# Block 2, the latents' attention: exponentials left undivided, outputs multiplied by reciprocal sums

## Chip, cores and metric

One NeuronCore of a Trainium2 chip runs the whole kernel. The metric is the device time of one execution in microseconds (us); three runs of the kernel before took 2768.22, 2770.35 and 2776.49, median 2770.35 us. Five engines matter: PE (TensorE, matrix products; PEld is its weight load), DVE (VectorE), ACT (ScalarE), POOL (GpSimd) and SP, whose queue issues most transfers.

## What is computed

Two blocks, each two layers deep, on 512 rows of width 1024. The change touches the second block's attention of the 512 latent rows: a windowed attention of 8 heads (A, with a sink logit) and a neighbourhood attention of 4 heads (B, with a bias), both also over 256 context keys.

```python
# A: window_gqa_latent, block of 128 queries
p = softmax(concatenate([s_win, s_ctx, s_sink], -1))
out = p[..., :span] @ vb + p[..., span:span+256] @ vc      # the sink only adds to the sum
# B: neighbourhood_latent
p = softmax(concatenate([s_nb, s_ctx], -1))
out = p[..., :n_keys] @ vr + p[..., n_keys:] @ vc
o = concatenate([o_a, o_b, o_c], -1) @ w_out               # o_c: a convolution branch
```

A row of p is exp(s - max) divided by its sum. Dividing the row of exponentials before the product with the values, or dividing the row of the output after it, gives the same output.

## The kernel before

The program is one straight instruction stream for each engine. A planner takes the program's operations, with costs and due times from a model of its own, and writes the order in which each engine gets them; every engine then works through its order. So two operations near each other in the text can stand far apart on an engine.

In block 2 each layer first projects the latent rows, then runs the latents' attention, then multiplies its output with `w_out` and goes on to the experts. The attention's output `oT` (printed as `mx` in the trace) is laid out transposed: chunk k holds the 64 channels of each of two heads on 128 partitions, 512 latents along the free axis. Chunks 0 to 3 are stage A (L1680 to L1719), chunks 4 and 5 stage B (L1726 to L1769), chunks 6 and 7 the convolution branch, whose taps (`conv_taps`, L862 and L865) and end (`conv_out`) are spread between.

Stage A runs over 4 pairs of heads `p_`, 4 tiles `t` of 128 latents and 2 heads `hh`: 32 heads' tiles a layer. `queries` (L1665, L1666) splits a pair's queries in two parts. A head's tile is: scores in PSUM (`scores`, `pa`, two buffers), the sink's column (L1699), `softmax_rows` into one of three `P` buffers, transposes by PE into `pt` (two buffers), copies to `PT`, and the products with the values into another `pt` tile, copied to `oT` (L1718). A tile has 513 columns (t = 0 and 3) or 641 (t = 1 and 2). Stage B runs over 2 pairs, 4 tiles and 2 heads: 16 heads' tiles a layer of 768 columns; L1749 adds the bias and takes the maximum.

`softmax_rows` takes the row maximum (L468), the exponential with its sum (L471, ACT; the sum leaves by a small read of ACT's accumulator), the reciprocal (L473, DVE) and multiplies the row of P by it (`copy`, L135): in A always on DVE, in B on DVE for the first head and on POOL for the second (`EA`, `EB`).

`proj_out` turns each chunk of `oT` into two parts, `hTh` (L369, ACT) and `hTl` (L370, DVE), which PE multiplies with the weights. Products of chunk 5 have to wait for the last output copy of stage B. `pj` is a third pair of PSUM buffers, which projections, small transposes and `conv_out` use.

Of the kernel before, what the change touches and what calls it, by code (L numbers as in the profile page):

```python
# [86 lines left out]
def _build(tc, nc, st, a, out):  # L87
# [38 lines left out]
    def copy(o, i, scale=None, eng=None):  # L126
        if eng is None:
            flip[0] ^= 1
            eng = "av"[flip[0]]
        if eng == "a":  # L130
            A.activation(o, i, AF.Copy, scale=1.0 if scale is None else scale)
        elif scale is None:
            V.tensor_copy(o, i)  # L133
        else:
            (G if eng == "g" else V).tensor_scalar(o, i, scale, None, op0=OP.mult)  # L135
# [11 lines left out]
    def pj():  # L147
        return cur["ps"].tile([128, 512], F32, tag="j", name="pj", bufs=2)
# [315 lines left out]
    def softmax_rows(S_, nh, lo, hi, P, ng=None, eng="v"):  # L464

        if ng is None:
            ng = small([128, nh], f"ng{nh}")
            V.tensor_reduce(ng, S_[:, :, lo:hi], axis=AX, op=OP.max, negate=True)  # L468
        su = small([128, nh], f"su{nh}")
        for i in range(nh):  # L470
            A.activation(P[:, i, lo:hi], S_[:, i, lo:hi], AF.Exp, bias=ng[:, i:i + 1], accum_out=su[:, i:i + 1])  # L471
        rc = small([128, nh], f"rc{nh}")
        V.reciprocal(rc, su)  # L473
        for i in range(nh):
            copy(P[:, i, lo:hi], P[:, i, lo:hi], rc[:, i:i + 1], eng)

    def heads2(x):
        return lambda hd: x[64 * (hd % 2):64 * (hd % 2) + 64, hd // 2, :]
# [973 lines left out]
    class Open:  # L1452
# [36 lines left out]
        def queries(self):  # L1489

            l, W, hcT = self.l, a["w_in_2"][self.l], self.hcT
            self.qa = self.crow().rearrange("p (a b) -> p a b", b=CTX)
            for j in range(2):
                w = wtile(W, 256 * j, 256)
                for b in range(2):
                    copy(self.qa[:, 2 * j + b, :], proj_T(w, hcT, CTX, b), 0.125)
            w = wtile(W, 768, 256)
            for b in range(2):
                copy(self.qb[:, b, :], proj_T(w, hcT, CTX, b), 0.125)
            conv_in(l, W, hcT, CTX, self.cglu, self.cpair)  # L1500
            bg.append(conv_taps(l, CTX, self.cglu, self.cacc))
            tick(8)
# [24 lines left out]
    for l in range(NL):  # L1527
# [152 lines left out]
        for p_ in range(4):  # L1680
            g = (2 * p_) // 4
            q_ = queries(qa[p_ // 2][:, p_ % 2, :])
            for t in range(4):
                c0, c1 = max(0, t - 1), min(3, t + 1)
                nw = c1 - c0 + 1
                lo = 512 - 128 * nw
                PT = ll.tile([128, 2, 4, 128], F32, tag="PT", name="PT", bufs=3)
                P5 = ll.tile([128, 2, 128], F32, tag="P5", name="P5", bufs=2) if nw == 3 else None
                tq = None
                for hh in range(2):  # L1690
                    hd = 2 * p_ + hh
                    s_ = pa().rearrange("p a b -> p (a b)")
                    scores(s_[:, lo:512], q_[:, hh, :], t, *part(kA, g, 128 * c0, 128 * c1 + 128), False)
                    if t > 0:
                        mm(s_[:, lo:lo + 128], identb, MB["left"], False, t == 3)
                    if t < 3:
                        mm(s_[:, 384:512], identb, MB["causal"], False, True)
                    scores(s_[:, 512:768], q_[:, hh, :], t, *part(kC, g, 0, CTX), True)
                    V.tensor_copy(s_[:, 768:769], sink[:, 8 * l + hd:8 * l + hd + 1])  # L1699
                    P = Pl()  # L1700
                    softmax_rows(s_[:, :776].unsqueeze(1), 1, lo, 769, P.unsqueeze(1), None, EA[(2 * t + hh) % len(EA)])
                    tp = pt()
                    for c in range(4):
                        tr(tp[:, 128 * c:128 * c + 128], P[:, lo + 128 * c:lo + 128 * c + 128])
                    copy(PT[:, hh, 0:4, :].rearrange("p c q -> p (c q)"), tp, eng="a")
                    if nw == 3:
                        if tq is None:
                            tq = pt()
                        tr(tq[:, 128 * hh:128 * hh + 128], P[:, lo + 512:lo + 640])
                if nw == 3:  # L1710
                    copy(P5, tq[:, :256].rearrange("p (h q) -> p h q", h=2))
                o_ = pt()
                for i in range(nw + 2):
                    for hh in range(2):
                        vv = va[:, c0 + i, 64 * g:64 * g + 64] if i < nw else vca[:, i - nw, 64 * g:64 * g + 64]
                        mm(o_[64 * hh:64 * hh + 64, :128], vv, PT[:, hh, i, :] if i < 4 else P5[:, hh, :], i == 0, i == nw + 1,
                           tile_position=(0, 64 * hh))
                copy(oT[:, p_, 128 * t:128 * t + 128], o_[:, :128])  # L1718
                tick(1)  # L1719
        if last:  # L1720
            qb = late_q()
            kb, vb = late()
# [3 lines left out]
        for p_ in range(2):  # L1726
            tb = [row4()[:, :960].rearrange("p (r c) -> p r c", c=64) for _ in range(2)]
            for r in range(2):
                for hh in range(2):
                    if r:  # L1730
                        G.memset(tb[hh][64:128, 0, :], 0.0)
                    src = bass.AP(natr.tensor, natr.offset + ((l * 4 + 2 * p_ + hh) * 15) * 8192 + 63,
                                  [[127, 64], [8192, 15 - r], [1, 64]])
                    nc.sync.dma_start(tb[hh][64 * r:64 * r + 64, r:15, :], src)
            for hh in range(2):
                G.tensor_tensor(out=tb[hh], in0=tb[hh],
                                in1=C["nacol"].unsqueeze(1).to_broadcast([128, 15, 64]), op=OP.add)
            q_ = queries(qb[:, p_, :])
            kB = keys(kb[:, p_, :], nbk[:, 4 * p_:4 * p_ + 2, :], nbk[:, 4 * p_ + 2:4 * p_ + 4, :])
            kC = keys(kcb[:, p_, :], *kparts(CTX, "BC"[p_]))  # L1740
            for t in range(4):
                PT = [ll.tile([128, 8, 128], F32, tag="PT", name="PT", bufs=3) for _ in range(2)]
                for hh in range(2):
                    hd = 2 * p_ + hh
                    s_ = pa().rearrange("p a b -> p (a b)")
                    scores(s_[:, 0:512], q_[:, hh, :], t, *part(kB, hh, 0, S), True)
                    scores(s_[:, 512:768], q_[:, hh, :], t, *part(kC, hh, 0, CTX), True)
                    m2 = small([128, 2], "m2")
                    V.tensor_tensor_reduce(out=s_[:, 0:512], in0=s_[:, 0:512],  # L1749
                                           in1=tb[hh][:, 7 - 2 * t:15 - 2 * t, :].rearrange("p r c -> p (r c)"),  # L1750
                                           scale=1.0, scalar=-3e38, op0=OP.add, op1=OP.max, accum_out=m2[:, 0:1])
                    V.tensor_reduce(m2[:, 1:2], s_[:, 512:768], axis=AX, op=OP.max)
                    ng = small([128, 1], "ngd")
                    V.tensor_reduce(ng, m2, axis=AX, op=OP.max, negate=True)
                    P = Pl()
                    softmax_rows(s_[:, :776].unsqueeze(1), 1, 0, 768, P.unsqueeze(1), ng, EB[(2 * t + hh) % len(EB)])
                    for i in range(2):
                        tp = pt()
                        for c in range(3):
                            tr(tp[:, 128 * c:128 * c + 128], P[:, 384 * i + 128 * c:384 * i + 128 * c + 128])  # L1760
                        copy(PT[hh][:, 3 * i:3 * i + 3, :].rearrange("p c q -> p (c q)"), tp[:, :384], eng="av"[i])
                o_ = pt()
                for c in range(6):
                    for hh in range(2):
                        hd = 2 * p_ + hh
                        vv = vb[:, c, 64 * hd:64 * hd + 64] if c < 4 else vcb[:, c - 4, 64 * hd:64 * hd + 64]
                        mm(o_[64 * hh:64 * hh + 64, :128], vv, PT[hh][:, c, :], c == 0, c == 5,
                           tile_position=(0, 64 * hh))
                copy(oT[:, 4 + p_, 128 * t:128 * t + 128], o_[:, :128])  # L1769
        pop()  # L1770
        conv_out(l, S, acc, oT, 6, lambda: (t4(), t4()))
        pop()
# [50 lines left out]
```

## Time and profile before

| | us |
|---|---|
| median of three runs | 2770.35 |
| profiled execution, its own time | 2777.7 |
| its span in the trace | 2775.9 |
| PE busy / PE weight loads busy | 2406.4 / 1439.1 |
| DVE busy | 1224.7 |
| ACT busy | 801.2 |
| POOL busy | 508.8 |

The four stretches in which the changed code runs are, from the span's start: A of the first layer 1100 to 1177 us, B of the first layer 1177 to 1236, A of the second layer 2036 to 2145, B of the second layer 2145 to 2203. They are 303 us of the span. A line of the trace gives an operation's line in the kernel, its engine, the tile written <- the tiles read; PE's products of the helper `mm` all have line L151, PE's transposes L160, the copies of `copy` L131 (ACT) and L133 or L135 (DVE, POOL).

### The profile page before, as it was taken

The page shows a single profiled execution, that of the slowest core. Times are in us where ns is not written, and L with a number is a line of the kernel's source. Part 1 is how long each engine was busy: PE and PEld are TensorE (multiplying, and loading weights), DVE is VectorE, ACT ScalarE, POOL GpSimd, SP SyncE. Part 2 cuts the span into 40 slices and gives each one's busy share as a digit, 9 for nine tenths or more (in the row PEclk, how much of TensorE's full clock was granted, in tenths as well). Part 3 has the DMA queues.
Part 4 walks back from the last instruction along what each step waited for, and adds up shares of the span by engine and source line. Part 5 has one row for each costly group of instructions (what it writes and reads, how often), then busy time and mean ns, then how long its engine had stood idle before and what let it go on. Part 6 is the DMA issues. An engine that isn't in the chain of part 4 may idle for free.

```text
span 2775.9 us, 39464 instructions
## 1 busy us (share of the span) xinstructions
PE 2406.4 (87%) x16255; PEld 1439.1 (52%) x16255; DVE 1224.7 (44%) x2367; ACT 801.2 (29%) x1522; POOL 508.8 (18%) x389
## 2 busy tenths in 40 slices
PE   6988889988998887995999999995798959988887
PEld 5765667655677665774333333334576733333323
DVE  4423554423666977866010101028778661112213
ACT  3353332363334434742101010103337420000001
POOL 3101222011233234042001010104322420000001
PEclk9999999999999997997999999998999969999998
DMA  5353562354444124035899999982221459999996
GB/s 179 116 169 120 164 182 84 107 184 141 133 134 153 61 99 128 8 131 212 355 393 349 419 341 420 340 337 100 68 68 30 160 207 410 421 420 421 421 421 233
DMA packets 216746, 613.17 MB, mean 221 GB/s; under 512 B 37592, under 2 KB 110830, under 8 KB 170486
## 3 DMA queue, kind: packets, MB, share of 16 engines
q1 hardware_dynamic: 207142, 576.74, 55.8%
q0 software_dynamic: 5440, 20.45, 2.6%
q10 hardware_dynamic: 3984, 13.45, 1.2%
q8 instruction: 128, 2.10, 0.3%
q14 instruction: 52, 0.43, 0.0%
HBM read 581.92 MB, written 28.67 MB: 220 GB/s over the span
## 4 chain that ended last, share of the span: by engine, by line
PE 35%; DVE 13%; DMA 11%; issue 8%; ACT 2%; POOL 2%; DVEq 0%; POOLq 0%; ACTq 0%; SPq 0%
PE pm L151 20%; PE pj L151 5%; PE pa L151 5%; DMA w<-in_w_up_dram 4%; DMA w<-in_w_gate_dram 4%; DVE acc L865 3%; DMA w<-in_w_down_dram 2%; PE pt L151 2%; PE pt L160 1%; DVE wl L331 1%; PE ptm L160 1%; DVE s L245 1%; POOL lnst L249 1%; ACT P L471 1%; DVE ng L468 1%
## 5 line engine op out<-in xcount | busy, mean ns | idle before, releaser
L151 PE MATMUL pm<-w,q 128*64 128x512 f32 (+1 forms) x1600 | 359.5, 597 | 40.3 <-DMA w<-in_w_up_dram 27.6
L151 PE MATMUL pm<-w,xT 128*32 128x512 f32 x3072 | 338.7, 599 | 0.0
L151 PEld LDWEIGHTS pm<-w,q 128*64 128x64 f32 x1600 | 122.6, 141 | 265.3 <-issue 200.5
L329 ACT ACTIVATE wh<-w 128x1024 fp32r<-128x1024 f32 (+2 forms) x154 | 161.3, 1050 | 317.2 <-PE pj L151 106.7
L331 POOL TENSOR_TENSOR wl<-w,wh 128x1024 fp32r<-128x1024 f32 (+1 forms) x57 | 143.5, 2520 | 464.0 <-ACT wh L329 448.0
L151 PE MATMUL pj<-hTh,wh 128*128 128x512 f32 x512 | 215.8, 422 | 13.3 <-ACT ty L301 7.2
L151 PEld LDWEIGHTS pm<-w,xT 128*32 128x32 f32 x3072 | 104.4, 111 | 228.1 <-issue 223.6
L151 PE MATMUL pj<-hTl,wh 128*128 128x512 f32 x512 | 207.7, 406 | 0.0
L151 PE MATMUL pj<-hTh,wl 128*128 128x512 f32 x512 | 206.1, 406 | 0.0
L151 PE MATMUL pm<-w,hid 128*32 128x512 f32 x1536 | 178.5, 593 | 0.0
L331 DVE TENSOR_TENSOR wl<-w,wh 128x1024 fp32r<-128x1024 f32 (+2 forms) x97 | 132.4, 1366 | 102.7 <-ACT wh L329 102.1
L1276 DVE TENSOR_TENSOR q<-pm,q 128x512 f32<-128x512 f32 x24 | 16.6, 692 | 285.6 <-PE pm L151 285.6
L160 PE MATMUL pt<-ident,P 128*128 128x128 f32 x712 | 121.2, 290 | 13.0 <-DVE mx L133 4.8
L151 PE MATMUL pa<-wh,hTh 128*128 128x512 f32 x256 | 106.3, 416 | 22.4 <-DVE ty L963 15.1
L1276 DVE TENSOR_TENSOR ty<-pm,ty 128x512 f32<-128x512 f32 x16 | 11.1, 691 | 256.4 <-PE pm L151 256.4
L151 PEld LDWEIGHTS pj<-hTh,wh 128*128 128x128 f32 x512 | 100.7, 197 | 40.5 <-issue 8.9
L1180 POOL DMA_INDIRECT q<-rowsl,idx x16 | 15.4, 960 | 563.0 <-PE ptm L160 432.7
L151 PEld LDWEIGHTS pj<-hTh,wl 128*128 128x128 f32 x512 | 99.5, 194 | 26.0 <-issue 3.3
L151 PEld LDWEIGHTS pj<-hTl,wh 128*128 128x128 f32 x512 | 100.2, 196 | 24.7 <-issue 4.2
L468 DVE TENSOR_REDUCE ng<-pa 128x1 f32<-128x513 f32 (+5 forms) x124 | 93.4, 756 | 35.1 <-PE pa L151 33.1
L151 PEld LDWEIGHTS pm<-w,hid 128*32 128x32 f32 x1536 | 50.4, 110 | 112.5 <-issue 110.7
L865 DVE SCALAR_TENSOR_TENSOR acc<-glu,vec,acc 128x512 f32<-128x512 f32 x120 | 108.6, 946 | 0.1
(447 smaller groups left out, 4465.3 us busy)
## 6 DMA issues: line engine op xcount, KB each, us to landing
w<-in_w_gate_dram SPq DMA_DIRECT2D x128, 1024.0 KB
w<-in_w_up_dram SPq DMA_DIRECT2D x127, 1024.0 KB
w<-in_w_down_dram SPq DMA_DIRECT2D x118, 1024.0 KB
w<-in_w_mod_dram SPq DMA_DIRECT2D x96, 512.0 KB
w<-in_w_in_dram SPq DMA_DIRECT2D x94, 512.0 KB
w<-in_w_out_dram SPq DMA_DIRECT2D x40, 512.0 KB
w<-in_w_down_dram SPq DMA_DIRECT2D x16, 512.0 KB
z<-q ACTq DMA_DIRECT2D x8, 512.0 KB
```

The source lines that it names most:

```text
L151: return T.matmul(o, l, r, start=start, stop=stop_, skip_group_check=True, **kw)
L160: T.transpose(o, i, ident[: i.shape[0], : i.shape[0]])
L245: pin(V.bn_stats(s6[:, c, :], x[:, c * w:c * w + w]))
L249: pin(G.tensor_tensor(out=rs, in0=ve, in1=mhalf[:, :n], op=OP.pow))
L329: A.activation(hi, w, AF.Copy)
L331: (lo_eng or (G if lot[0] % 3 == 0 else V)).tensor_tensor(out=lo, in0=w, in1=hi.bitcast(F32), op=OP.subtract)
L468: V.tensor_reduce(ng, S_[:, :, lo:hi], axis=AX, op=OP.max, negate=True)
L471: A.activation(P[:, i, lo:hi], S_[:, i, lo:hi], AF.Exp, bias=ng[:, i:i + 1], accum_out=su[:, i:i + 1])
L865: V.scalar_tensor_tensor(acc[:, c, :n], glu[:, c, tap:tap + n], w, acc[:, c, :n], op0=OP.mult, op1=OP.add)
L1180: pin(G.indirect_dma_start(out=r, out_offset=None, in_=s["rows"][:], in_offset=bass.IndirectOffsetOnAxis(ap=s["idx"][:, i:i + 1], axis=0)) ...
L1276: V.tensor_tensor(out=x, in0=up[b][h], in1=x, op=OP.mult)
```

## The change

`softmax_rows` is replaced in both latents' stages by `exp_rows`, which does the maximum and the exponential alone and leaves the sum in one column of a small tile `su` of the pair. P stays undivided through the transposes and the products with the values. After a pair's four tiles `over_sums` takes the reciprocals of its eight columns of sums, spreads each over the 64 partitions of its head with a product (the stationary operand is a column of reciprocals repeated 64 times, the moving one the 128x128 unit matrix) into a `pj` tile, and multiplies the pair's chunk of `oT` with it in place. `EA` and `EB` no longer matter. The other attentions of the kernel keep `softmax_rows`.

```diff
+    def exp_rows(S_, lo, hi, P, ng, su):
+        if ng is None:
+            ng = small([128, 1], "ng1")
+            V.tensor_reduce(ng, S_[:, lo:hi], axis=AX, op=OP.max, negate=True)
+        A.activation(P[:, lo:hi], S_[:, lo:hi], AF.Exp, bias=ng, accum_out=su)
+
+    def over_sums(su, o):
+        rc = small([128, 4, 2], "rcp", bufs=2)
+        V.reciprocal(rc, su)
+        p = pj()
+        for t in range(4):
+            for hh in range(2):
+                mm(p[64 * hh:64 * hh + 64, 128 * t:128 * t + 128], rc[:, t, hh:hh + 1].to_broadcast([128, 64]), ident,
+                   True, True, tile_position=(0, 64 * hh))
+        V.tensor_tensor(out=o, in0=p, in1=o, op=OP.mult)
...
             q_ = queries(qa[p_ // 2][:, p_ % 2, :])
+            su = small([128, 4, 2], "suq", bufs=3)
...
-                    softmax_rows(s_[:, :776].unsqueeze(1), 1, lo, 769, P.unsqueeze(1), None, EA[(2 * t + hh) % len(EA)])
+                    exp_rows(s_, lo, 769, P, None, su[:, t, hh:hh + 1])
...
                 tick(1)
+            over_sums(su, oT[:, p_, :])
...
             q_ = queries(qb[:, p_, :])
+            su = small([128, 4, 2], "suq", bufs=3)
...
-                    softmax_rows(s_[:, :776].unsqueeze(1), 1, 0, 768, P.unsqueeze(1), ng, EB[(2 * t + hh) % len(EB)])
+                    exp_rows(s_, 0, 768, P, ng, su[:, t, hh:hh + 1])
...
                 copy(oT[:, 4 + p_, 128 * t:128 * t + 128], o_[:, :128])
+            over_sums(su, oT[:, 4 + p_, :])
```

## Rows read from the trace of the kernel before

**Rows 1.** Stretches: length, busy us (count) of PE, PEld, DVE, ACT, POOL; clock, DMA share, GB/s

```profile
1100.00:1177.00 77.00, 69.18 (x637) 54.58 (x636) 67.72 (x200) 52.40 (x122) 10.38 (x11) 0.94 0.07 14
1177.00:1236.00 59.00, 54.00 (x450) 42.93 (x446) 44.55 (x130) 30.58 (x63) 26.26 (x22) 1.00 0.21 67
2036.00:2145.00 109.00, 97.40 (x764) 80.04 (x764) 84.89 (x193) 65.80 (x140) 21.54 (x19) 0.95 0.22 48
2145.00:2203.00 58.00, 53.31 (x441) 42.50 (x442) 43.46 (x125) 30.39 (x63) 26.52 (x22) 1.00 0.21 69
```

**Rows 2.** Chain of waits, shares by line: first layer's A and B, second layer's A

```profile
by line: PE pa L151 21.6%; PE pt L151 16.1%; ACT P L471 12.1%; DVE ng L468 10.1%; DVE P L135 9.5%; PE pt L160 9.3%; issue 2.1%; DVE Q L1666 1.8%; DVE q L885 1.7%; DVE af L1054 1.4%; DVE rc L473 1.3%; DVE pa L1699 1.3%; ACT PT L131 1.3%; DVE
by line: PE pa L151 35.8%; PE pt L151 20.4%; PE pt L160 13.2%; DVE pa L1749 6.8%; issue 5.1%; DVE PT L133 4.4%; ACT hTh L369 2.2%; ACT P L471 2.0%; ACT q L887 1.7%; ACT PT L131 1.7%; DVE m L1752 1.4%; DVE P L135 1.2%; DVE q L885 1.0%; ACT m
by line: PE pj L151 27.0%; PE pa L151 18.4%; PE pt L151 13.0%; PE pt L160 9.3%; ACT P L471 5.6%; DVE P L135 5.4%; DVE ng L468 4.5%; DVE Q L1666 3.7%; issue 2.5%; DVE nbk L1648 2.3%; ACT PT L131 1.4%; PE pj L160 1.2%; DVE q L885 1.2%; DVE pa
```

**Rows 3.** Waits of PE: for whom, us in total, times, longest; first layer's A, B

```profile
PE pa L151 <- ACT P L471: 3.0, 8, 0.6
PE pj L160 <- DVE af L1054: 2.8, 1, 2.8
...
PE pt L160 <- DVE PT L133: 1.5, 4, 0.6
PE pa L151 <- ACT hTh L369: 1.0, 1, 1.0
```

**Rows 4.** Groups of instructions, first layer's A and B: busy, mean ns | idle before

```profile
L135 DVE TENSOR_SCALAR P<-P,rc 128x513 f32<-128x513 f32 x16 | 10.8, 676 | 0.4
L135 DVE TENSOR_SCALAR P<-P,rc 128x641 f32<-128x641 f32 x16 | 8.8, 551 | 0.5
L135 DVE TENSOR_SCALAR P<-P,rc 128x768 f32<-128x768 f32 x8 | 6.3, 782 | 0.2
L473 DVE RECIPROCAL rc<-su 128x1 f32<-128x1 f32 x48 | 7.4, 154 | 2.3 <-ACT P L471 1.7
...
L135 POOL TENSOR_SCALAR P<-P,rc 128x768 f32<-128x768 f32 x8 | 17.7, 2210 | 15.6 <-DVE rc L473 6.6 <-DVE ngd L1754 5.3 <-PE pt L151 2.2
```

**Rows 5.** Order of time at a change of pair in A: start, us, engine

```profile
1135.83 0.49 DVE L135 TENSOR_SCALAR P<-P,rc 128x513 f32<-128x513 f32 x1
1136.35 0.69 DVE L1666 TENSOR_TENSOR Q<-q,Q 64x512 fp32r<-64x512 f32 x1
1137.06 0.29 DVE L133 COPY mx<-pt 128x128 f32<-128x128 f32 x1
1137.41 0.88 PE L160 MATMUL pt<-ident,P 128*128 128x128 f32 x6 [0.18 <-DVE mx L133]
1138.61 0.39 PE L151 MATMUL pa<-KA,Q 128*128 128x256 f32 x1 [0.32 <-ACT P L471]
```

**Rows 6.** Order of time in A: DVE beside POOL

```profile
1143.15 2.24 POOL L1736 TENSOR_TENSOR q<-q,cst 128x960 f32<-128x960 f32 x1 [4.81 <-DMA q<-natr]
1143.23 2.44 DVE L135 TENSOR_SCALAR P<-P,rc 128x513 f32<-128x513 f32 x1
```

**Rows 7.** Order of time in the output product: DVE beside POOL

```profile
1243.56 2.52 POOL L964 TENSOR_TENSOR q<-q,ty 128x512 f32<-128x512 f32 x2
1243.92 0.69 DVE L963 TENSOR_TENSOR ty<-pa,q 128x512 f32<-128x512 f32 x1 [1.75 <-PE pa L151]
```

**Rows 8.** Order of time in A: bursts of PE, value products and transposes

```profile
1121.40 0.88 PE L151 MATMUL pt<-PT,va 128*64 128x128 f32 x12
1122.64 0.66 PE L160 MATMUL pt<-ident,P 128*128 128x128 f32 x4
```

**Rows 9.** Order of time at the end of B, first layer

```profile
1234.67 0.28 ACT L131 ACTIVATE mx<-pt 128x128 f32<-128x128 f32 x1 [2.25 <-PE pt L151]
1234.98 0.63 ACT L369 ACTIVATE hTh<-mx 128x512 fp32r<-128x512 f32 x1
1235.66 0.50 PE L151 MATMUL pa<-wh,hTh 128*128 128x512 f32 x1 [1.03 <-ACT hTh L369]
```

## Prediction before the run

> **What bounds the kernel now.** The change lives in four stretches that the windows of the trace bound: A and B of the first layer, 77 and 59 us, A and B of the second, 109 and 58 us, 303 us together [rows 1]. I read the busy times of these windows first. PE has something in flight for 69.18 of 77 us, 54.00 of 59, 97.40 of 109 and 53.31 of 58, that is 89 to 92%, 273.9 us in all; what it leaves empty is 7.8, 5.0, 11.6 and 4.7 us, 29.1 us. DVE is the second engine: 67.72 of 77 us (88%) in the first layer's A, 75 to 78% in the other three. ACT has 50 to 70%, POOL 14 to 46%.
>
> The second view is the chain of waits in these windows [rows 2]. Products and transposes of PE are the largest part of it, but in the first layer's A DVE's division of P (L135) carries 9.5%, its reciprocal (L473) 1.3% and the maximum (L468) 10.1%. In the second layer's A the division carries 5.4%, and the projections that are mixed in there (`pj`) 27.0%. In B it is 1.2%. The third view is PE's own list of waits [rows 3]: nowhere among its longer ones does PE wait for the division itself. It waits for the exponential that frees a score buffer (3.0 us in 8 waits in the first layer's A), for a copy of transposed P, for the last chunk before the output product (1.0 us). So DVE sits on the path through what stands behind the division in its order, not through P arriving late.
>
> **What the change removes.** In one layer 40 divisions on DVE, 10.8 + 8.8 + 6.3 = 25.9 us, and 48 reciprocals, 7.4 us [rows 4]; 33.3 us a layer, 66.6 us in two layers if the second costs the same. On POOL 8 divisions of 2210 ns, 17.7 us a layer. Most of that lies beside PE's work and is worth nothing. What can come back at most is what stands on the chain: (9.5 + 1.3)% of 77 = 8.3 us in the first layer's A, 5.4% of 109 = 5.9 in the second's, 1.2% of 59 = 0.7 in each B: 15.6 us. B's chain also has 5.1% of "issue", 3.0 us, of which a part can be a division that DVE holds without getting on; with all of it in both layers the upper end is 21.6 us. The lower end is 0, since PE is at 89 to 92%.
>
> Which value? At a change of pair in A the division of 0.49 us stands in front of the split of the next queries (0.69) and the output copy (0.29), and PE's transposes start when that copy is done [rows 5]. With reciprocal and division gone the copy comes about 0.6 us earlier. But PE showed waits of only 0.18 us in front of these transposes and 0.32 in front of the next scores: what is late next is PE's own work. So I don't take the whole chain: three quarters where DVE is at 88% (6.2 of 8.3), half in the second layer's A, where the projections fill PE (3.0 of 5.9), and all of B (1.4). Gain: 10.6 us.
>
> A division can cost far more than its 0.48 us: one took 2.44 us while POOL added the bias tables for 2.24 us, and both ended almost together [rows 6]. That is one of the places where the chain's 8.3 us come from. The Trainium skill says why (SBUF — State Buffer, section "SBUF: two separate sides"): DVE in a two-port mode and POOL take one pair of ports in turn, and the loser is held for the whole instruction; rows and page agree. The new multiplication reads one operand from PSUM, and an addition of that form took 0.69 us while POOL was busy for 2.52 us [rows 7], so I price it at 0.69 without such a wait.
>
> **What the change adds.** Six pairs a layer, 12 in all, each with one reciprocal of 8 columns, 8 products and one multiplication of 128x512.
>
> PE: the products have the shape of the value products (64 stationary columns, 128 moving ones, the two halves of the array in turn). Twelve of those took 0.88 us, 0.073 each; four transposes, which can't go in pairs, 0.66, 0.165 each [rows 8]. A set of 8 is then 0.59 us by the nearer row and 1.32 by the farther, 7.0 or 15.8 us for 12 sets. A stationary operand that repeats one column 64 times is in no row; its load is priced with the burst, as one of 64 different columns, and the farther row is the end if it is not. The lower end is 0, because PE leaves 29.1 us empty. The sets come due at the changes of pair, where PE does wait [rows 5], so I count half of the nearer value: 3.5 us. What is queued behind them on PE are the next pair's scores; they would wait for the reciprocal only if the planner put the set ahead of the last value products, since the sums are there before P has been transposed.
>
> DVE: 12 times (0.154 + 0.69) = 10.1 us against 66.6 removed, nothing on the path in A and between B's pairs, where 0.69 us go into the time made free. At the end of B there is no cover: the last output copy ends at 1234.95, and the cast for the output product starts at 1234.98 [rows 9], with PE idle for 1.03 us until it is done. The multiplication goes in between, 0.69 us and two hand-overs of 0.03: 0.75 a layer, 1.5 us in all. If reciprocal and products come late too, 0.15 + 0.59 more, 3.0 us in all; if PE has other products left, 0.
>
> ACT: exponentials and copies stay. POOL's 35.4 us in two layers go, which no one replaces. No transfer is moved. `pj` gets 12 more tiles; its other users in these stretches are few in the first layer and the projections in the second.
>
> **Sum.** -10.6 + 3.5 + 1.5 = -5.6 us. The profiled execution took 2777.7 us (its span 2775.9 and 1.8 around it), so it would be 2772.1; the median of the three runs, 2770.35, is 7.35 lower, and minus 5.6 it is 2764.75. I forecast 2765.
>
> **Rivals.** (a) The path in these stretches is the chain through DVE and not PE. PE's weight loads are busy for 54.58 of 77 us [rows 1], 71%, so the 89% may be products waiting to drain. Then what leaves the chain comes back whole, 15.6 us or a little more as POOL stops holding DVE, against 1.5 for the ends and next to nothing for products in empty time: -14 to -16 us, 2755. Against it: PE's list of waits is short [rows 3]. On this the Trainium skill (Perfetto Trace Analysis, section "Identifying the Most-Contended Engine") says that busy products are a bad measure of how close PE is to its limit, and weight-load busy time a good one; by that rule the room is 29% and not 11, and this rival holds. The trace bears it out in part.
>
> (b) Slower: PE is the limit, and what DVE gives back is spent waiting for PE. Then the gain is small, and 12 sets of 8 products stand in PE's order in full, 7.0 us by the nearer row and 15.8 by the farther, with 3.0 at the ends: 10 to 18.8 us less perhaps 2 that still comes back, +8 to +17; 2780. It decides from the point where less than 5 us come back. For it speaks PE's 92% in both B [rows 1]; against it that the sets fall where PE waits.
>
> (c) Nothing moves: division off the path, products in empty time, end covered or 1.5 us. 2769 to 2772. Since the planner writes a new order for every engine, a few us of either sign go with each case.
>
> **How the numbers follow.** Forecast (2760 to 2770) 0.45, (a) 0.22, (b) 0.15, (c) 0.18. About 0.3%, 8.3 us, is what a measurement of this kernel can tell from no change: faster is below 2762, slower above 2778.7. Faster: nearly all of (a) and a quarter of the forecast, 0.33. Slower: two thirds of (b) and a little of the new order, 0.13. The same: 0.54. The range: 2750 takes in (a) with the upper end of the chain, 2779 half of (b): 2750 to 2779.
>
> **What would show it.** Right, if in the changed profile: L135 is gone from these stretches and DVE's busy time is down by some 56 us in them; the product sets take about 0.6 us and stand where PE waited before; the division's share of the chain has gone to PE; the four stretches are 3 to 8 us shorter in sum, most of it in the first layer's A; from the last value product of B to the output product's next step it is about 0.7 us longer. Wrong, if PE's busy share rises to 95% and the stretches are no shorter (b), if they are over 12 us shorter (a), or if the time changes in stretches that hold none of the changed code.

## The result, and the profile after

The changed kernel takes 2858.07 us (median, 2852.82 to 2864.52); the kernel before, run beside it, 2771.68. The ratio is 1.0312, 95% interval 1.0296 to 1.0328: slower by 3.1%, 86 us. Forecast were 2765, between 2750 and 2779.

The profiled span is 2857.4 us against 2775.9, +81.5. Where it lies can be read from the exponentials (P written by ACT) and from the hand-over between the layers (the first store of `x_d`). Times are from each span's start.

| | before | after | added |
|---|---|---|---|
| first layer, first exponential of A to last of B | 1102.4 to 1220.1 | 1101.4 to 1218.5 | -0.6 |
| last exponential of B to the hand-over | to 1914.9 | to 1947.7 | +34.4 |
| hand-over to first exponential of A, second layer | to 2038.0 | to 2066.6 | -4.2 |
| second layer, first exponential of A to last of B | to 2187.1 | to 2236.4 | +20.7 |
| last exponential of B to the end | to 2775.9 | to 2857.4 | +32.2 |

With the -1.0 by which A starts earlier these make 81.5. So the first layer's attention, where the forecast looked, takes as long as before, and the loss lies behind B in both layers and in the second layer's attention. The stretches of A and B of the first layer, and two new ones behind B, one in each layer (columns as in [rows 1]):

```profile
1098.00:1175.00 77.00, 70.45 (x659) 56.16 (x658) 49.15 (x132) 52.69 (x122) 9.00 (x10) 0.94 0.08 14
1175.00:1236.00 61.00, 55.51 (x498) 45.83 (x497) 38.32 (x102) 28.43 (x59) 1.10 (x2) 1.00 0.04 10
1243.00:1272.00 29.00, 4.67 (x30) 2.78 (x28) 5.55 (x13) 3.26 (x4) 10.23 (x14) 0.58 0.94 378
2262.00:2288.00 26.00, 3.94 (x24) 2.37 (x24) 4.62 (x11) 2.24 (x4) 10.25 (x14) 0.55 1.00 400
```

DVE falls from 67.72 to 49.15 us of 77 in A and from 44.55 to 38.32 in B [rows 1]; PE's time rises by 1.3 us and, in 61 us instead of 59, by 1.5. In the two new stretches nearly everything stands still: PE has something in flight for 4.67 of 29 us and 3.94 of 26, while the DMA engines are at 94 to 100%. The chain of waits names what is waited for, in the first layer and in the second (start us, us, what):

```profile
1245.11 11.72 DMA w<-in_w_gate_dram
1256.85 14.81 DMA q<-mod
...
1271.75 0.70 DVE ty L981
...
2155.09 12.31 PE pj L151 x51
...
2171.80 8.77 DMA q<-natr
...
2262.75 11.18 DMA w<-in_w_gate_dram
2273.94 13.86 DMA q<-mod
```

L981 is the output product's multiplication with the row of `mod` (the line that was L963 in [rows 7]): it waits for a row of 0.5 MB, whose load is itself issued only when a load of the experts' gate weights has landed. The two pieces of 2155 and 2171 us lie between A and B of the second layer: the projections of B's queries, keys and values, which filled A before [rows 2], and the bias tables (`natr`), issued from 2170.2 us instead of 2068.1. The issues on SP's queue, first layer: kernel before, then changed kernel (line, engine, transfer, count: ns of the issue, first and last start):

```profile
L1775 SPq DMA_DIRECT2D q<-x_d x4: 319/344/425, 1191.7 to 1194.3; - x4
L894 SPq DMA_DIRECT2D q<-mod x1: 320/320/320, 1212.2 to 1212.2; - x1
L1158 SPq DMA_DIRECT2D w<-in_w_gate_dram x11: 327/544/830, 1234.6 to 1280.0; - x11
```

```profile
L1176 SPq DMA_DIRECT2D w<-in_w_gate_dram x7: 346/425/848, 1243.8 to 1247.2; - x7
L1797 SPq DMA_DIRECT2D q<-x_d x4: 319/324/489, 1247.7 to 1254.3; - x4
L912 SPq DMA_DIRECT2D q<-mod x1: 320/320/320, 1256.8 to 1256.8; - x1
```

The order is turned round: seven loads of 1 MB now stand ahead of `x_d` and `mod`, and `mod` is issued 45 us later. What SP's issues waited for, from 1243 to 1264 us of the changed kernel (line, for what: us in total, times, longest):

```profile
SPq L1176 <- PE pj L160: 12.7, 1, 12.7
SPq L912 <- DMA w<-in_w_gate_dram: 7.4, 3, 3.1
SPq L1797 <- DMA w<-in_w_gate_dram: 5.5, 3, 2.6
```

The gate loads (L1176) waited for a transpose of the convolution (`pj`, L160), and then `x_d` and the rows waited for gate loads to land. The trace's records show how: the loads of these stretches take eight semaphores (counters that a landing transfer raises) in turn, `mod` stands on that of the fourth gate load, and it was issued when that one had landed, at 1256.8 us. `mod` itself then took 14.8 us to land, where it took 4.0 in the kernel before, with no gate load in flight. The other thing that has moved is the end of the convolution branch. Its first transposes (`pj<-ident,acc`), first layer and second, before and then after:

```profile
L160 PE MATMUL pj<-ident,acc x8: 270/272/273, 1119.2 to 1180.5; 128*128 128x128 f32 x8
L160 PE MATMUL pj<-ident,acc x8: 270/272/421, 2089.3 to 2147.5; 128*128 128x128 f32 x8
```

```profile
L160 PE MATMUL pj<-ident,acc x8: 272/300/418, 1226.8 to 1243.5; 128*128 128x128 f32 x8
L160 PE MATMUL pj<-ident,acc x8: 272/300/421, 2244.7 to 2261.1; 128*128 128x128 f32 x8
```

Before, they ran between A's tiles; now they run behind B's last set of products, whose last one starts at 1226.6 us in the first layer. The chain's shares answer [rows 2] (A and B of the first layer): the division (L135) and its reciprocal (L473) are gone, PE has what was theirs, and the new products (`pj L151`) have 4.6 and 5.3%.

```profile
by line: PE pa L151 34.0%; PE pt L151 24.6%; PE pt L160 18.2%; ACT P L482 7.6%; PE pj L151 4.6%; ACT Q L1683 1.6%; DVE af L1072 1.4%; issue 1.4%; DVE LB L1666 1.1%; DVE Q L1684 0.9%; DVE ng L481 0.8%; ACT KC L1663 0.7%; ACT PT L131 0.6%; PE
by line: PE pa L151 36.4%; PE pt L151 21.6%; PE pt L160 15.3%; DVE pa L1770 5.8%; PE pj L151 5.3%; DVE PT L133 4.9%; issue 3.2%; DVE wl L331 1.9%; ACT P L482 1.6%; DVE q L903 1.2%; DVE mx L493 1.1%; PE pj L160 1.0%; DVE m L1770 0.7%; ACT mx
```

The new operations over the whole span, and then the end of B in order of time (which answers [rows 9]):

```profile
L151 PE MATMUL pj<-ident,rcp 128*64 128x128 f32 x192 | 14.8, 279 | 0.4 <-DVE rcp L487 0.4
L493 DVE TENSOR_TENSOR mx<-pj,mx 128x512 f32<-128x512 f32 x12 | 8.3, 692 | 4.5 <-ACT mx L131 4.5
```

```profile
1235.40 0.28 ACT L131 ACTIVATE mx<-pt 128x128 f32<-128x128 f32 x1 [3.14 <-PE pt L151]
1235.71 0.69 DVE L493 TENSOR_TENSOR mx<-pj,mx 128x512 f32<-128x512 f32 x1 [0.53 <-ACT mx L131]
...
1236.44 0.63 ACT L369 ACTIVATE hTh<-mx 128x512 fp32r<-128x512 f32 x1 [0.76 <-DVE mx L493]
```

96 products show as 192 instructions of PE, two for each. The multiplication takes the 0.69 us that it was priced at, and the cast comes 0.76 us later than it would.

**The theory after the result.** The buffers of one PSUM tag are handed out in the order of the text, whatever order the planner writes: `pj` has two, so a tile cannot be written before the one two places ahead of it in the text is done with. The six new `pj` tiles of a layer stand ahead of `conv_out`'s in the text, and in the second layer the four of A also stand ahead of the late projections of stage B's queries, keys and values. So these can no longer run between A's tiles. I call this theory R (ring). It has a second link, the queue: with the convolution late, the planner's order for SP puts the gate weights ahead of `x_d` and `mod`. There are two rivals, named as in the expectations: W (work), that the products and the multiplication themselves cost the 86 us, and P (order), that without the divisions the planner writes a worse order whatever buffer is used.

### The profile page after: what moved, and what is told of

It reads as the page before. It is cut to its first block, busy times and chain, and to the rows that moved or that the text cites. A ratio compares the mean times of both kernels' runs of the same rounds, so it can differ in the third digit from the quotient of the medians.

```text
span 2857.4 us, 39701 instructions
## 1 busy us (share of the span) xinstructions
PE 2431.0 (85%) x16447; PEld 1458.9 (51%) x16447; DVE 1189.7 (42%) x2215; ACT 803.3 (28%) x1522; POOL 475.6 (17%) x373
## 4 chain that ended last, share of the span: by engine, by line
PE 35%; DVE 12%; DMA 11%; issue 7%; ACT 2%; POOL 2%; SPq 0%; DVEq 0%; POOLq 0%; ACTq 0%
PE pm L151 20%; PE pa L151 5%; PE pj L151 4%; DMA w<-in_w_up_dram 4%; DMA w<-in_w_gate_dram 4%; DVE acc L883 3%; PE pt L151 2%; DMA w<-in_w_down_dram 2%; PE pt L160 2%; DMA q<-mod 1%; DVE c L883 1%; DVE wl L331 1%; PE ptm L160 1%; DVE s L245 1%; ACT P L482 1%
## 5 line engine op out<-in xcount | busy, mean ns | idle before, releaser
L151 PE MATMUL pm<-w,q 128*64 128x512 f32 (+1 forms) x1600 | 357.0, 594 | 42.2 <-DMA w<-in_w_up_dram 29.6
L151 PE MATMUL pm<-w,xT 128*32 128x512 f32 x3072 | 338.9, 598 | 0.0
L151 PEld LDWEIGHTS pm<-w,q 128*64 128x64 f32 x1600 | 122.3, 141 | 265.1 <-issue 198.6
L151 PE MATMUL pj<-hTh,wh 128*128 128x512 f32 x512 | 214.6, 420 | 9.5 <-ACT wh L329 4.9
L151 PEld LDWEIGHTS pm<-w,xT 128*32 128x32 f32 x3072 | 104.3, 111 | 228.4 <-issue 223.8
L151 PE MATMUL pj<-hTl,wh 128*128 128x512 f32 x512 | 208.0, 407 | 0.0
L151 PE MATMUL pj<-hTh,wl 128*128 128x512 f32 x512 | 204.9, 404 | 0.0
L151 PE MATMUL pm<-w,hid 128*32 128x512 f32 x1536 | 178.5, 593 | 0.0
L151 PE MATMUL pa<-wh,hTh 128*128 128x512 f32 x256 | 111.5, 437 | 62.0 <-DVE ty L981 47.2
L160 PE MATMUL pt<-ident,P 128*128 128x128 f32 x712 | 122.0, 291 | 30.2 <-ACT P L482 17.6
L151 PEld LDWEIGHTS pj<-hTh,wh 128*128 128x128 f32 x512 | 100.3, 196 | 37.0 <-ACT wh L329 5.8
L151 PEld LDWEIGHTS pj<-hTl,wh 128*128 128x128 f32 x512 | 100.0, 195 | 24.1 <-issue 3.9
L160 PEld LDWEIGHTS pt<-ident,P 128*128 128x128 f32 x712 | 82.0, 145 | 58.7 <-issue 20.8
L151 PEld LDWEIGHTS pj<-hTh,wl 128*128 128x128 f32 x512 | 98.4, 192 | 25.6 <-issue 3.8
L151 PE MATMUL pa<-wl,hTh 128*128 128x512 f32 x256 | 109.3, 428 | 0.0
```

What stands on the lines that cost most here:

```text
L151: return T.matmul(o, l, r, start=start, stop=stop_, skip_group_check=True, **kw)
L160: T.transpose(o, i, ident[: i.shape[0], : i.shape[0]])
```

## Experiments

All times are medians, ratios are to the kernel before on the same chip in the same stretch of time.

**1. The same products in another ring (e1_pt).** `pt` is used only inside A and B.

```diff
-        p = pj()
+        p = pt()
```

> The changed kernel with one word changed: the spread products write a `pt` buffer instead of a `pj` buffer. Theory R (ring): the 86 us come from the place of the product tile. Buffers of one tag are handed out in the order of the text, two `pj` tiles in turn; six new `pj` tiles a layer stand ahead of the convolution's end and, in the second layer, ahead of the late projections, which before could run inside A and B. They now wait for the sums of the last pair, and transfers behind them change places. Then this kernel falls to 2755 to 2775 us, conv_out's transposes run inside A and B again, and the experts' first weights stand behind the residual rows in SP's order. Rival W (work): the loss is the added products and multiplications themselves on PE and DVE, 12 sets. Then it stays at 2840 to 2865. Rival P (order): without the divisions the planner writes another order whatever buffer is used. Then it stays above 2830 too.

Measured: 2780.06 us, ratio 1.0031 (1.0017 to 1.0045). The tag is worth 78 of the 86 us. (R's range, 2755 to 2775, is missed by 5 us.) The queue's old order is back, with `mod` ahead of the gate weights:

```profile
L912 SPq DMA_DIRECT2D q<-mod x1: 320/320/320, 1211.0 to 1211.0; - x1
L1176 SPq DMA_DIRECT2D w<-in_w_gate_dram x11: 328/471/698, 1233.3 to 1280.5; - x11
```

W and P fall for nine tenths of the loss. What is left, 8 us, is still slower than before and not the gain that was forecast.

**2. The kernel before with sets added (e2_ones_pj, e2_ones_pt).** The divisions stay; twelve sets run on a tile of ones.

```diff
+    ones8 = con.tile([128, 4, 2], F32, name="ones8")
...                                                   # over_sums, as in the change
+            over_sums(ones8, oT[:, p_, :])        # in A, and the same in B
```

> The kernel before with its divisions kept, and after each pair the new set on top of it (reciprocal, 8 products into a `pj` tile, multiplication of the chunk), fed with sums of one, so that nothing is changed in value. Theory R: the `pj` tiles alone bring the loss, 2850 to 2875 us. Rival W: also 2850 and up. Rival P: the loss needs the divisions to be gone, so 2772 to 2790.

> The same as the kernel before with sets of ones on top, but with the products in a `pt` tile. Theory R: only the added work is left, priced at 3.5 for PE and 1.5 for the ends: 2772 to 2785 us. Rival W: as with `pj`, 2850 and up. Rival P: 2772 to 2790.

Measured: 2836.09 us in `pj`, ratio 1.0224 (1.0199 to 1.025); 2788.7 in `pt`, 1.0062 (1.0045 to 1.0079). With the softmax unchanged and only the sets added, the kernel is far above P's 2790: the loss does not need the divisions to be gone. Of the 62 us (by the ratio) only 17 are left in `pt`, which rules out W. R's figures are missed too, 2850 by 14 us and 2785 by 4: the tag is worth 45 us here and not 78. One reason shows in the queue: here five gate loads stand ahead of `x_d` and not seven, and `mod` is issued 7.5 us after the first of them (1248.4 us) and not 13.1. In `pt` the sets alone cost 17 us, where the forecast's sum had 5.

**3. The division taken away, nothing in its place (e3_nodiv).**

```diff
-            over_sums(su, oT[:, p_, :])
...
-            over_sums(su, oT[:, 4 + p_, :])
```

> The changed kernel without over_sums: exponentials undivided, and nothing in place of the division, which is left out, so the attention's outputs are not normalised. It measures the gain alone, priced at 10.6 us (0 to 21.6). Theory R: 2750 to 2770 us. Rival W: 2750 to 2770 too. Rival P: above 2830, since the divisions are gone.

Measured: 2766.21 us, ratio 0.999 (0.9973 to 1.0006). This is all that the change could give back: 2.8 us by the ratio, 7.5 at the end of its interval, against 10.6 in the sum. P, which had this kernel above 2830, is out. Its first layer's A (columns as in [rows 1]) and one of PE's waits in it:

```profile
1102.00:1178.00 76.00, 69.53 (x640) 55.12 (x639) 50.19 (x142) 52.91 (x123) 10.57 (x13) 0.94 0.08 14
```

```profile
PE pa L151 <- ACT P L482: 2.0, 6, 0.4
```

DVE does 17 us less in A than in [rows 1]. PE's wait for the exponential falls from 3.0 to 2.0 us [rows 3]. From the first exponential of A to the last of B it is 115.5 us instead of 117.7, in the second layer 149.4 against 149.1. (Both traces are of long executions of their kernels, 2776.01 and 2777.7 us.) This also decides the forecast's rival (a). The Trainium skill (Perfetto Trace Analysis, "Identifying the Most-Contended Engine"), weighed in the forecast, would leave PE 29% of room in A by its weight-load time; the room could not be used, the 17 us of DVE brought about 2.

**4. Which of the products hold what (e4_a_pj_b_pt, e5_a_pt_b_pj).** The tag is chosen for each stage.

```diff
-            over_sums(su, oT[:, p_, :])
+            over_sums(su, oT[:, p_, :], pj)       # e5: pt
...
-            over_sums(su, oT[:, 4 + p_, :])
+            over_sums(su, oT[:, 4 + p_, :], pt)   # e5: pj
```

> The changed kernel with the four product tiles of stage A in pj and the two of stage B in pt. Theory R (the buffers of pj go round in the order of the text, so a tile that stands later in the text cannot be used before the new one is done): only what stands after A in the text and would run in it is held, which is the second layer's late projections (stage B's own pj tiles) and the bias tables that wait for their q4 tiles. The output convolution of block 2 stands after the last pj tile of A, so it may start once A is over. On e1_pt's 2780 that adds the +16 us net which the second layer's late projections cost in the changed kernel: 2790 to 2805, with the rows of x_d ahead of the experts' gate weights on SP's queue in both layers. A rival, that each set costs more in pj than in pt by a wait of its own (4 of 6 sets lie in A): two thirds of 78 us, 2825 to 2840.

> The changed kernel with the four product tiles of stage A in pt and the two of stage B in pj. Theory R: the late projections run inside A as before, but the output convolution's pj tiles stand behind B's last product, so it moves to the end of B in both layers, frees its q4 tiles late, and the experts' gate weights get ahead of x_d and mod on SP's queue. On e1_pt's 2780 that adds the +33 us of the first layer's end and the +32 of the second's: 2835 to 2850. The rival of a price for each set in pj (2 of 6 sets): a third of 78 us, 2800 to 2812.

Measured: A in `pj` 2801.7 us, ratio 1.0122 (1.009 to 1.0154); B in `pj` 2837.65, ratio 1.0244 (1.0213 to 1.0275). Both fall where R put them, and neither where a price for each set would (2825 to 2840, 2800 to 2812): the two sets of B cost more than twice as much as the four of A. The traces put the loss where R does. Against e1, e5 loses 30 and 33 us behind B of the two layers and e4 nothing there (-1 and -3); the second layer's attention, from the first exponential of A to the last of B, takes 174.6 us in e4 and 152.6 in e5, beside 155.3 in e1. SP's queue in the first layer, e4 and then e5:

```profile
L912 SPq DMA_DIRECT2D q<-mod x1: 319/319/319, 1209.4 to 1209.4; - x1
L1176 SPq DMA_DIRECT2D w<-in_w_gate_dram x11: 328/442/745, 1231.8 to 1278.9; - x11
```

```profile
L1176 SPq DMA_DIRECT2D w<-in_w_gate_dram x7: 347/424/842, 1240.9 to 1244.3; - x7
L912 SPq DMA_DIRECT2D q<-mod x1: 320/320/320, 1253.5 to 1253.5; - x1
```

The convolution's transposes begin at 1170.0 us in e4, where A's last set begins its last product at 1169.8, and at 1225.6 in e5, where B's last set does so at 1225.4.

**5. A third ring (e6_pa).** The set in `pa`, the ring of the scores.

```diff
-        p = pj()
+        p = pa()[:, 0, :]
```

> The changed kernel with the product tiles in pa, the ring of the scores and of the outputs, which nothing outside A and B uses in these stretches. Theory R: nothing is held, 2775 to 2795, as e1_pt within the cost of one more turn of pa's buffers for each of the 12 sets (0 to 1.3 us each). The rival, that the cost of the change lies in the products and multiplies whatever their tag: 2845 to 2865.

Measured: 2823.69 us, ratio 1.02 (1.0168 to 1.0232). A miss: I had priced one turn of the buffers, but the same rule holds in `pa`. The next pair's scores stand behind the set in that ring, so PE can't do them ahead of time: in e6 the next pair's first scores start at 1114.2, 1135.0 and 1155.3 us, 1 us after the sets of 1113.2, 1134.0 and 1154.3, while in e1 four of the next pair's eight have started before the set of 1120.7 (1111.9 to 1119.0). The two attentions are 16.8 and 13.0 us longer than in e1, 30 of the 47 us between the two; the rest is not explained. PE's waits from 1093 to 1235 us, e6 and then e1:

```profile
PE pt L160 <- ACT P L482: 8.2, 5, 3.2
PE pt L151 <- ACT P L131: 5.3, 4, 2.2
```

```profile
PE pa L151 <- ACT P L482: 3.6, 10, 0.6
PE pt L160 <- DVE PT L133: 2.5, 4, 0.7
```

**6. The rows issued from ACT's queue (e7_act_queue).** In `rows_of` and for `x_d`, products in `pj`.

```diff
-            nc.sync.dma_start(x, bc_src(src, off, D))
+            nc.scalar.dma_start(x, bc_src(src, off, D))
...
-            nc.sync.dma_start(xs[t], x_d[128 * t:128 * t + 128, :])
+            nc.scalar.dma_start(xs[t], x_d[128 * t:128 * t + 128, :])
```

> The changed kernel, products in pj as there, but the loads of x_d and of the rows (mod, ln_g, ln_b) are issued from ACT's queue and not from SP's. The queue link of theory R (after the output convolution comes late, mod's row waits behind seven 1 MB loads of the gate weights, some 26 us of stall in each layer): the stall mostly goes, 2800 to 2830, with the late convolution (+9 a layer) and the second layer's late projections (+16) left. The rival, that the convolution itself being late makes the stall and the queue only shows it: above 2845. A chance of its own against both: loads issued by ACT stand in ACT's order and wait there, which could hold the exponentials; the chain would then show ACT issuing ahead of them.

Measured: 2853.51 us, ratio 1.0303 (1.0267 to 1.0338): by the ratios 2.5 us better than the changed kernel, not 28 to 58. By its own words that spoke for the rival, that the convolution's lateness makes the stall. The trace shows that the run could not tell. On ACT the loads of `x_d` stand behind the late convolution's tanh (L905). And the other queue did not free `mod` from the gate loads, which SP issued from 1242.9 us on: it still shares a semaphore with the fourth of them, issued at 1244.3, and goes out when that one lands (ACT's order, then the chain of waits):

```profile
1248.60 1.06 ACT L905 ACTIVATE q<-q 128x1024 f32<-128x1024 f32 x1 [5.05 <-DVE q L903]
1248.73 5.19 ACTq L1797 DMA_DIRECT2D q<-x_d  x4
```

```profile
1244.27 12.93 DMA w<-in_w_gate_dram
1257.22 12.51 DMA q<-mod
```

Nor did a queue of their own make the transfers themselves much quicker: `mod` landed 12.5 us after its issue, beside 14.8 in the changed kernel, and in both some 11 MB moved at 380 GB/s between 1243 and 1272 us. The Trainium skill (DMA: Bandwidth & Descriptors, "Issuing engines are not separate DMA queues") says that transfers of all issuing engines run on the same 16 DMA engines and interleave; the trace agrees.

**7. The gate weights held until `mod` is there (e11_gate_after_mod).** Products in `pj`, the convolution late, only the order of the queue is mended.

```diff
+        if n == S:
+            G.tensor_copy(hold, gm[:, 0:1])              # behind the row of mod
...
+            if loads[0] < 7:
+                G.tensor_copy(w[:, 0, 0:1], hold)        # ahead of a gate weight's load
```

> The changed kernel, products in pj, but the first seven loads of the experts' gate weights in each layer must wait until mod's row has landed (a small POOL copy from that row into each of their tiles), so x_d and mod go first on SP's queue and have the DMA engines for themselves; the convolution stays late. If the stall of some 26 us a layer is the seven 1 MB loads ahead of x_d and mod (order of the queue and the shared engines), most of it goes, mod lands before 1252 us, and the gate weights come some 10 us later, which the experts may give back: 2810 to 2835. If the stall comes from the late convolution, which frees the rows' buffers late, mod still lands after 1262 us and the time is 2850 or more.

Measured: 2823.78 us, ratio 1.0198 (1.0174 to 1.0223); 1.14 of 3.12%, 32 of 86 us by the ratios, are back; what the two intervals leave open is about 8 us. By the traces, whose first layer's A starts 9.5 us earlier here with the same code ahead of it, the two stretches behind B are 11 and 12 us shorter than in the changed kernel, 24 us together. SP's queue, and then the stretch from 24.5 us behind B's last exponential on, 29 us long, as that of 1243 us in the changed kernel:

```profile
L1802 SPq DMA_DIRECT2D q<-x_d x4: 319/400/591, 1220.9 to 1222.4; - x4
L913 SPq DMA_DIRECT2D q<-mod x1: 320/320/320, 1224.8 to 1224.8; - x1
L1181 SPq DMA_DIRECT2D w<-in_w_gate_dram x11: 327/423/831, 1247.0 to 1288.9; - x11
```

```profile
1232.90:1261.90 29.00, 16.04 (x68) 11.29 (x67) 16.30 (x21) 4.33 (x5) 17.04 (x26) 0.71 0.60 231
```

PE has something in flight for 16.04 us, where it had 4.67. `x_d` is issued at 1220.9 us, 12 us ahead of the convolution's last first transpose (1233.1), and `mod` at 1224.8, landing 6.1 us later. So their buffers don't wait for the convolution (only the row of `ln_g`, issued at 1241.4, waits for its last step). What held `x_d` and `mod` back in the changed kernel was their place behind the gate loads, which were themselves held by the late convolution until 1243.8. The queue link holds, and my first wording of it, in the expectation of e5, that the late convolution frees the rows' buffers late, is wrong for these. Against e1 some 21 us a layer are left behind B; the late convolution and the gate loads, which here go out later still, are not told apart in them. The chip sees only the order; why the planner turns it round when the convolution is late is not shown.

**8. The other users moved ahead in the text (e8_conv_first, e9_both_first).** Products in `pj`.

```diff
         drain()
+        conv_out(l, S, acc, oT, 6, lambda: (t4(), t4()))    # was behind stage B
...
```

and in e9 also `late_q()` and `late()` ahead of A's loop.

> The changed kernel, products in pj as there, but the call of block 2's output convolution stands in the text ahead of stage B and not behind it; nothing else differs. Theory R (a ring's tiles are used in the order of the text): the convolution's pj tiles no longer stand behind B's two products, so it may run from the end of A on as in e4_a_pj_b_pt; x_d and mod are loaded ahead of the gate weights, and only the second layer's late projections, which stand behind A's four products, are still held: 2795 to 2810, as e4's 2801.7. Rival, that pj's products cost by being in pj, wherever the other users stand: 2845 or more, no better than the changed kernel.

> As e8_conv_first, and the second layer's late projections (late_q and late) stand in the text ahead of stage A's loop as well; products in pj. Theory R: nothing stands behind the products any more but themselves, so pj costs what pt costs: 2770 to 2795 around e1_pt's 2780; the first A of the second layer may start some 5 to 12 us later, as the projections stand ahead of it, and its end come earlier by as much. Rival: 2800 or more, something else in pj holds.

Measured: 2818.4 us, ratio 1.0181 (1.0161 to 1.0201), and 2809.63, ratio 1.015 (1.0124 to 1.0177). The direction is R's, by the ratios 36 and 45 us better than the changed kernel with the products still in `pj`, but both miss their figures, by 8 and 15 us; e9's, by its own words, speaks for the rival that something else in `pj` holds. The traces say what is left: the convolution no longer fills gaps but stands in one piece between A and B. Its chain of small steps ends in the tanh and DVE's step behind it (L906); only then does DVE come to B's first step (L1771), for which B's first exponential waits. Between A's last exponential (1170.6) and B's first (1194.5) lie 24 us in e8, where the kernel before has 4, and in e9 it is 24 us in both layers. Against e1, e9 is 16 and 18 us longer in the two attentions and not longer behind B, together the 33 us that the ratios leave between the two: the gaps account for it, and nothing else in `pj` is needed.

```profile
1189.30 1.06 ACT L905 ACTIVATE q<-q 128x1024 f32<-128x1024 f32 x1 [9.29 <-DVE q L903]
1190.39 2.79 DVE L906 SCALAR_TENSOR_TENSOR mx<-q,q 128x1024 f32<-128x1024 f32 x1 [1.12 <-ACT q L905]
1193.10 0.69 DVE L1771 CUSTOM_DVE_ANT_0 pa<-pa,q 128x512 f32<-128x512 f32 x1
...
1194.52 0.90 ACT L482 ACTIVATE P<-pa,ngd 128x768 f32<-128x768 f32 x1 [0.17 <-DVE ngd L1776]
```

**9. Sets of half as many instructions (e10_pt_bf16).** e1 with reciprocals and unit matrix in bf16.

```diff
-        rc = small([128, 4, 2], "rcp", bufs=2)
+        rc = small([128, 4, 2], "rcp", BF16, bufs=2)
...
-                mm(..., rc[:, t, hh:hh + 1].to_broadcast([128, 64]), ident,
+                mm(..., rc[:, t, hh:hh + 1].to_broadcast([128, 64]), identb,
```

> e1_pt with the reciprocals and the unit matrix of the spreading products in bf16 (coarser reciprocals; nothing left out). What is tested is the term for one set: in e1_pt a set of 8 products shows as 16 PE instructions in 1.02 us. If a set's price is PE's time, 8 instructions of about 0.06 us remain, 0.5 us less for each of 12 sets, and with PE the limit in A and B most of that comes back: 2773 to 2776. If a set's price is the wait of the chain reciprocal, products, multiply (some 2 us of order at a head pair's end), nothing comes back: 2779 to 2782.

Measured: 2770.34 us, ratio 1.002 (1.0002 to 1.0038), on a chip on which the kernel before took 2766.15, where it had taken 2771.77 beside e1. By the ratios it is 3 us better than e1, which put beside e1's 2771.77 makes 2777, between the two figures expected; and the intervals overlap. The traces are clearer. One set, e1 and then e10:

```profile
1120.69 0.27 PE L151 MATMUL pt<-ident,rcp 128*64 128x128 f32 x1
1120.80 1.14 PE L151 MATMUL pt<-ident,rcp 128*64 128x128 f32 x15
```

```profile
1119.49 0.28 PE L151 MATMUL pt<-identb,rcp 128*64 128x128 bf16 x2
1119.60 0.49 PE L151 MATMUL pt<-identb,rcp 128*64 128x128 bf16 x6
```

From the first exponential of A to the last of B the two layers take 115.5 and 149.4 us in e3 without sets, 122.3 and 155.3 in e1, 118.7 and 151.2 in e10. Twelve sets cost 12.7 us in fp32 and 5.0 in bf16, 1.06 and 0.42 each (by the ratios, e1 is 11 us above e3). A set costs about what PE takes for it (1.04 to 1.25 us in e1, 0.39 to 0.60 in e10), and hardly any of the fp32 sets' time is hidden: from e3 to e1 PE's busy time in the two layers rises by 11.9 us. That the first layer's attention is no longer than before in the changed kernel, 117.1 us, does not speak against this: there the convolution has left it.

## Why the prediction was wrong

**The step that failed** is the last sentence on what the change adds: "No transfer is moved. `pj` gets 12 more tiles; its other users in these stretches are few in the first layer and the projections in the second." I named the shared ring and its users, and took their number for their price. What counts is where the new tiles stand in the text against them. Those few users were `conv_out`, and with it late the loads changed places and waited for one another. In the second layer I had the projections in the chain of A at 27.0% [rows 2], work that fills A only as long as it may run there. The 78 us between the changed kernel and e1 are all this step's. e4 gives A's sets 25 us of it (0.0122 - 0.0031 of 2771.5), e5 gives B's 59; that is 84 together, the same within the intervals. Of the whole, the order of the loads is 24 us by the traces and 32 by the ratios (e11).

The forecast's own list had the sign of it: "if the time changes in stretches that hold none of the changed code".

**The gain.** 10.6 us in the sum, 2.8 by e3's ratio, not told from zero. The step that was mis-sized is the share of the chain: I took three quarters of 8.3 us in the first layer's A and half of 5.9 in the second's; 2.2 us came back from the first layer's A and B together, and nothing in the second. When L135 and L473 left the chain, PE's transposes and products took their place, and the room that they left was PE's own work. Of my bounds (0 to 21.6) e3's interval leaves nothing beyond 7.5.

**The sets.** 0.59 us each, half of it hidden, 3.5 us; measured 1.06 each, 12.7. Two steps failed. The nearer row was the value products at 0.073 us each [rows 8], but there twelve instructions are six products, since an fp32 product shows as two: 8 products are 16 instructions, and 16 at 0.073 make 1.17, close to the 1.04 to 1.25 measured. And nothing was hidden, because the waits at the change of pair that I counted on are short [rows 5].

**The ends.** 0.75 us a layer was right: 0.76 [rows 9]. The multiplication was right too, 0.692 against 0.69. DVE's fall was smaller than the 56 us named: between the first exponential of A and the last of B it is 44.6 us in e1 (226.1 to 181.5, both layers).

**The rivals.** With the ring out of the way the sum would have been -2.8, +12.7 for the sets and +1.5 for the ends, about +11; e1 is 8 to 9 us above the kernel before. That is rival (b), PE as the limit, with +8 to +17. That its figure of 2780 is met by 2780.06 is luck, within so wide a range. So even there the sign was wrong: e1 lies at the bound of what can be told from no change, on the slow side, where I had given 0.13, and not on the fast one, with 0.33. Rival (a) is ruled out by e3. No rival held the reversal of the queue.

No version that was run beats the kernel before. e3, which has no price at all, is 0.1% below it with an interval that takes in zero, so undivided exponentials have nothing measurable to give here.

## What to carry to other kernels

Before adding a tile to a shared PSUM or SBUF tag, list that tag's users in the order of the text and look in the trace for those that run earlier than the text has them: the new tile pins them behind itself, and whatever they feed. Then look at what the queue does when they are late, since a small row behind 7 MB of weights costs a stall of its own, and look at what its issue waits for before giving it another queue. And count instructions from rows of the same data type: where PE is the limit, nearly every one of them is paid.

## What the runs showed of the hardware

An fp32 product of 64 stationary and 128 moving columns stands in the trace as two PE instructions, the same product in bf16 as one; a set of eight took 1.04 to 1.25 us in e1 and 0.39 to 0.60 in e10. In the two stalls the granted clock of TensorE is 0.58 and 0.55 on average, which is near the lower of its two levels (1.2 and 2.4 GHz), while PE has something in flight for a sixth of the time; in the stretch ahead of the first one, B, it is 1.00. And with the 16 DMA engines full, a row of 0.5 MB took 12.5 to 14.8 us from issue to landing, on SP's queue behind the weights as on ACT's queue beside them; with no gate load in flight it took 4.0 in the kernel before and 6.1 in e11.
